# RMSNorm on one core: tiles two to four loaded whole, the first tile's store cut at row 1 and the second's at row 4

## The chip, the cores and the metric

The kernel runs on one core of a Trainium2 chip. The metric is the time of one execution on the device in microseconds (us). Three runs of the kernel before took 161.49, 161.64 and 162.53 us; the median, 161.64 us, is what the change is measured against.

The engines that matter here are ScalarE (ACT), VectorE (DVE), GpSimd (POOL), and SyncE (SP), which in this kernel does nothing but issue the transfers. All transfers go through SP's one queue to the core's 16 DMA engines. TensorE (PE) is used once, at the start.

## The reference

```python
def setup_inputs():
    batch, seq, dim = 16, 1024, 512
    return {
        "x": np.random.randn(batch, seq, dim).astype(np.float32),
        "gamma": np.ones(dim, dtype=np.float32),
    }

def reference(x: np.ndarray, gamma: np.ndarray) -> np.ndarray:
    eps = 1e-5
    rms = np.sqrt(np.mean(x ** 2, axis=-1, keepdims=True) + eps)
    return (x / rms * gamma).astype(np.float32)
```

Each of the 16,384 rows of 512 fp32 numbers is divided by its own root mean square and multiplied by gamma.

## The kernel before, in words

**Tiles, slots and rows.** The input is cut into four tiles of 128 partitions by 32 rows by 512 numbers, numbered 0 to 3 in the code ("the first tile" is tile 0). A partition holds 32 neighbouring rows of the input, so a tile is 64 KB in each partition. In what follows "a row" means one row in each of the 128 partitions: 256 KB. SBUF has room for three such tiles, `slot0` to `slot2`. The result is written over the input in place and stored from there. Tile 3 uses slot 0 again (`slot_of = [0, 1, 2, 0]`), so it can be loaded only when tile 0 has been stored. The profile does not tell slots or tiles apart: it writes `slot` for all three.

**Groups.** The list `groups` cuts the four tiles into nine groups of rows, (tile, first row, number of rows, pieces for the squares, rows given to POOL). A group's steps are these:

- `square_sums` (lines 96 and 97): ACT squares a piece of rows into scratch, DVE sums each row. Scratch is `sq_psum` (up to 7 rows) for even pieces, `sq_sbuf` (up to 5 rows) for odd ones. A piece of 9 rows goes to the last nine rows of slot 2 instead, which are free until tile 2 is loaded there.
- `inverse_rms` (lines 102 and 103): a square root on ACT, a reciprocal on DVE, for the whole group.
- `scale_by_pool` (lines 109 and 110): POOL multiplies the last rows of the group by the inverse and by gamma.
- `scale` (line 118): ACT multiplies the other rows by the inverse, one instruction a row, nine of a group of sixteen (thirteen in the last group).
- `times_gamma` (line 122): DVE multiplies these rows by gamma in one instruction.

**The order.** It is written out by hand; no scheduler changes it. The loop at the end works on group k and on the squares of group k+1 at once: on ACT the first two square pieces of the next group come first, then half of this group's scaling, then the third square piece if there is one, then the rest of the scaling. On DVE come the three sums of the next group, then `times_gamma` of this one, then the reciprocal of the next. Each engine runs its own list in order, so ACT, while it waits for data to square, does not scale the group before.

**Transfers.** `load` (line 45) and `store` (line 49) each issue one DMA on SP. SP runs its list in order too: a transfer whose wait is not over holds back all those behind it. Five loads are issued at the start (with gamma, in five small pieces, among them): tile 0 in rows 0:1, 1:8, 8:16 and 16:32, and the first half of tile 1. The others are issued by `transfers(t, g)`, called after `times_gamma` of group (t, g). A reader of loaded rows waits until the whole DMA that brings them has completed.

Of the kernel before, what the change touches and what calls it, by code (L numbers as in the profile page):

```python
# [9 lines left out]
def kernel(  # L10
# [33 lines left out]
    def load(t, slot, r0, r1):  # L44
        dma = nc.sync.dma_start(out=slots[slot][:, r0:r1], in_=xv[t][:, r0:r1])  # L45
        before_scale.append((slot, r0, r1, dma))

    def store(t, slot, r0, r1):
        dma = nc.sync.dma_start(out=ov[t][:, r0:r1], in_=slots[slot][:, r0:r1])
        before_scale.append((slot, r0, r1, dma))  # L50
# [6 lines left out]
    for c0, c1 in zip(pieces, pieces[1:]):  # L57
        nc.sync.dma_start(out=gamma_row[:, c0:c1], in_=gamma.unsqueeze(0)[:, c0:c1])
    load(0, 0, 8, 16)
    load(0, 0, 16, 32)  # L60
    load(1, 1, 0, 16)

    ones_col = const.tile([1, P], fp32)
    nc.gpsimd.memset(ones_col, 1.0)  # L64
# [11 lines left out]
    groups = [  # L76
        (0, 0, 7, (7,), 3),
        (0, 7, 9, (9,), 5),
        (0, 16, 16, (7, 9), 7),
        (1, 0, 16, (7, 9), 7),  # L80
        (1, 16, 16, (7, 5, 4), 7),
        (2, 0, 16, (7, 5, 4), 7),
        (2, 16, 16, (7, 5, 4), 7),
# [43 lines left out]
                tc.declare_no_dep(scaled.ins, earlier.ins, reason="ScalarE waited for it before it scaled these rows")  # L127

    def transfers(t, g):
        if (t, g) == (0, 0):  # L130
            store(0, 0, 0, 1)
            load(1, 1, 16, 32)
            store(0, 0, 1, 2)
            load(2, 2, 0, 23)
        elif (t, g) == (0, 16):
            store(0, 0, 2, 3)
            load(2, 2, 23, 32)
            store(0, 0, 3, 16)
            store(0, 0, 16, 32)
            load(3, 0, 0, 16)  # L140
            load(3, 0, 16, 32)
        elif (t, g) == (1, 16):
            store(1, 1, 0, 32)
        elif (t, g) == (2, 16):
            store(2, 2, 0, 32)
        elif (t, g) == (3, 0):
            store(3, 0, 0, 16)
        elif (t, g) == (3, 16):
            store(3, 0, 16, 32)
# [16 lines left out]
    for k, group in enumerate(groups):  # L166
        t, g, n, pieces, share = group
        mine = n - share
        half = (mine + 1) // 2
        ahead = groups[k + 1 :][:1]  # L170
        ss, todo = pieces_of(ahead[0]) if ahead else (None, [])
        scale_by_pool(rstd, t, g, n, share)
        for piece in todo[:2]:
            square_sums(*piece)
        scale(rstd, t, g, 0, half)
        for piece in todo[2:]:
            square_sums(*piece)
        scale(rstd, t, g, half, mine)
        times_gamma(t, g, 0, mine)
        transfers(t, g)  # L180
        for nxt in ahead:
            rstd = inverse_rms(ss, nxt[2])
# [30 lines left out]
```

## Time and profile before

| | |
|---|---|
| Median of three runs | 161.64 us |
| Span of the profiled execution | 160.2 us |
| DVE, ACT, POOL busy | 112.0, 107.8, 106.4 us |
| DMA queue of SP, packets and bytes | 2746, 67.11 MB |
| Its share of 16 DMA engines' span | 98.1% |
| Last DVE instruction ends | 139.1 us |
| Last store issued by SP, and its time to landing | 139.2 us, 20.1 us |

The span is the time from the first to the last instruction on the core in one profiled execution. The median of the runs is that of executions without a profile, and 1.4 us longer than the span. Only differences of the two kernels are compared, span with span, and the difference is laid on the median.

In the views that follow a line of the timeline has start, duration, engine, line of the code, operation, output <- input with shapes, and in brackets the idle time before it and what ended that. A line of several instructions (x4) has the time from the first one's start to the last one's end. A line of DMA issues has the number of transfers, KB of each, and microseconds from issue to landing where the profile could tell. For SP, the duration is that of issuing, not of the transfer.

### The profile page before, as it was taken

Reading aid. Unit: us, or ns where it says so; the run is one execution under the profiler, and the core shown is the slowest. Engines: PE = TensorE matmul, PEld = TensorE weight load, DVE = VectorE, ACT = ScalarE, POOL = GpSimd, SP = SyncE. Lnnn points to the kernel's source line nnn. Section 1 sums busy time; section 2 is a strip of 40 time slices with the busy share of each in tenths; the row PEclk is TensorE's granted clock in tenths of the full one; section 3 lists DMA queues with packets and bytes.
Section 4 is the critical chain, followed back from the end, with each engine's and each line's share of the span. In section 5 each row is a group of like instructions: output and inputs, shape, how many; then the busy total and the mean of one; then the engine's idle time right before and its main releaser. Section 6 shows DMA issues by size and latency. Waiting matters only on the chain.

```text
span 160.2 us, 276 instructions
## 1 busy us (share of the span) xinstructions
PE 2.0 (1%) x2; PEld 0.5 (0%) x2; DVE 112.0 (70%) x39; ACT 107.8 (67%) x108; POOL 106.4 (66%) x24
## 2 busy tenths in 40 slices
PE   0050000000000000000000000000000000000000
PEld 0010000000000000000000000000000000000000
DVE  0018098899798999999999999999999009700000
ACT  3071967976999998999899899989960990000000
POOL 1000951994999599999999999999999980000000
DMA  5999999899999899999999999996996996999994
GB/s 189 431 421 475 442 401 458 340 446 491 417 435 494 388 379 383 426 450 475 434 401 426 483 401 393 524 491 295 524 491 295 524 491 295 401 491 417 401 450 196
DMA packets 2747, 67.12 MB, mean 419 GB/s; under 512 B 313, under 2 KB 314, under 8 KB 826
## 3 DMA queue, kind: packets, MB, share of 16 engines
q1 hardware_dynamic: 2746, 67.11, 98.1%
q14 instruction: 1, 0.01, 0.0%
HBM read 33.56 MB, written 33.55 MB: 419 GB/s over the span
## 4 chain that ended last, share of the span: by engine, by line
DVE 59%; ACT 22%; DMA 4%; ACTq 0%; issue 0%; SPq 0%
DVE ss L97 36%; DVE slot L122 23%; ACT slot L118 8%; ACT slot L96 7%; ACT sq_psum L96 6%; DMA slot<-in_x_dram 4%; DVE ss L103 1%; ACT ss L102 1%; ACTq L208 0%; ACT gamma_b L165 0%; SPq L45 0%; ACTq L96 0%
## 5 line engine op out<-in xcount | busy, mean ns | idle before, releaser
L109 POOL TENSOR_TENSOR slot<-slot,ss 128x3584 f32<-128x3584 f32 (+2 forms) x9 | 47.0, 5218 | 24.1 <-DVE ss L103 24.1
L110 POOL TENSOR_TENSOR slot<-slot,gamma_b 128x3584 f32<-128x3584 f32 (+2 forms) x9 | 59.3, 6587 | 0.7
L97 DVE TENSOR_REDUCE ss<-sq_psum 128x7 f32<-128x3584 f32 (+1 forms) x13 | 42.2, 3247 | 13.7 <-ACT sq_psum L96 13.7
L118 ACT ACTIVATE slot<-slot,ss 128x512 f32<-128x512 f32 x75 | 47.3, 706 | 4.7 <-DVE ss L103 4.7
L122 DVE TENSOR_TENSOR slot<-slot,gamma_psum 128x4608 f32<-128x4608 f32 (+2 forms) x9 | 41.3, 4590 | 8.7 <-ACT slot L118 8.7
L96 ACT ACTIVATE sq_psum<-slot 128x3584 f32<-128x3584 f32 (+1 forms) x13 | 34.6, 2658 | 6.4 <-DMA slot<-in_x_dram 5.7
L97 DVE TENSOR_REDUCE ss<-slot 128x9 f32<-128x4608 f32 x3 | 14.9, 4954 | 4.4 <-ACT slot L96 4.2
L97 DVE TENSOR_REDUCE ss<-sq_sbuf 128x5 f32<-128x2560 f32 x5 | 14.0, 2803 | 0.0
L96 ACT ACTIVATE slot<-slot 128x4608 f32<-128x4608 f32 x3 | 12.1, 4033 | 0.0
L96 ACT ACTIVATE sq_sbuf<-slot 128x2560 f32<-128x2560 f32 x5 | 11.6, 2321 | 0.0
L102 ACT ACTIVATE ss<-ss,eps_t 128x16 f32<-128x16 f32 (+2 forms) x9 | 2.7, 305 | 11.9 <-DVE ss L97 11.9
L103 DVE RECIPROCAL ss<-ss 128x16 f32<-128x16 f32 (+2 forms) x9 | 2.1, 236 | 0.4 <-ACT ss L102 0.4
L66 PE MATMUL gamma_psum<-gamma_row,ones_col 1*128 1x512 f32 x2 | 2.0, 1122 | 8.6 <-DMA gamma_row<-in_gamma_dram 8.6
L72 ACT ACT_TABLE_LOAD x1 | 1.3, 1283 | 1.2 <-PEq L197 1.2
L165 ACT COPY gamma_b<-gamma_psum 128x512 f32<-128x512 f32 x1 | 0.6, 567 | 0.0
L66 PEld LDWEIGHTS gamma_psum<-gamma_row,ones_col 1*128 1x128 f32 x2 | 0.5, 308 | 8.6 <-issue 8.6
L64 POOL MEMSET ones_col<- 1x128 f32 x1 | 0.2, 195 | 0.3 <-POOLq L197 0.3
L197 POOL MEMSET const-float32-0.0<- 128x1 f32 x1 | 0.1, 99 | 0.2 <-issue 0.2
L72 ACT ACTIVATE table<-eps_t 128x1 f32<-128x1 f32 x1 | 0.2, 202 | 0.0
L197 POOL MEMSET const-bfloat16-1.0<- 128x1 bf16 x1 | 0.1, 102 | 0.0
L197 POOL MEMSET const-uint8-127<- 128x1 uint8 x1 | 0.1, 102 | 0.0
L197 POOL MEMSET const-float32-1.0<- 128x1 f32 x1 | 0.1, 99 | 0.0
(1 smaller groups left out, 0.1 us busy)
## 6 DMA issues: line engine op xcount, KB each, us to landing
slot<-in_x_dram SPq DMA_DIRECT2D x5, 4096.0 KB, 21.9
out_dram<-slot SPq DMA_DIRECT2D x3, 4096.0 KB, 23.4
slot<-in_x_dram SPq DMA_DIRECT2D x1, 5888.0 KB
out_dram<-slot SPq DMA_DIRECT2D x1, 3328.0 KB, 21.8
slot<-in_x_dram SPq DMA_DIRECT2D x1, 2304.0 KB, 14.3
slot<-in_x_dram SPq DMA_DIRECT2D x1, 2048.0 KB, 9.9
slot<-in_x_dram SPq DMA_DIRECT2D x1, 1792.0 KB, 7.0
out_dram<-slot SPq DMA_DIRECT2D x3, 256.0 KB
```

The costliest lines, as they stand in the source:

```text
L66: nc.tensor.matmul(gamma_psum[:, 0], ones_col, gamma_row, start=True, stop=True)
L72: nc.scalar.activation(out=table, in_=eps_t, func=AF.Sqrt)
L96: nc.scalar.activation(out=sq[:, :m], in_=rows, func=AF.Square)
L97: nc.vector.tensor_reduce(out=ss[:, r : r + m, 0], in_=sq[:, :m], axis=mybir.AxisListType.X, op=OP.add)
L102: nc.scalar.activation(out=ss[:, :n, 0], in_=ss[:, :n, 0], func=AF.Sqrt, bias=eps_t, scale=1.0 / D)
L103: nc.vector.reciprocal(out=ss[:, :n, 0], in_=ss[:, :n, 0])
L109: nc.gpsimd.tensor_tensor(out=part, in0=part, in1=by_row, op=OP.mult)
L110: last = nc.gpsimd.tensor_tensor(out=part, in0=part, in1=gamma_b.to_broadcast([P, share, D]), op=OP.mult)
L118: nc.scalar.activation(out=x[:, g + r, :], in_=x[:, g + r, :], func=AF.Copy, scale=rstd[:, r])
L122: scaled = nc.vector.tensor_tensor(out=part, in0=part, in1=gamma_psum.to_broadcast([P, r1 - r0, D]), op=OP.mult)
L165: nc.scalar.copy(out=gamma_b[:, 0], in_=gamma_psum[:, 0])
L197: nc = _bacc.Bacc("TRN2", target_bir_lowering=False, num_devices=1)
```

## The change

- The pair of half loads of tile 1, the two pieces of tile 2's load (rows 0:23 and 23:32) and the two half loads of tile 3 become one load of 32 rows each. Tile 1's load stays in the list at the start.
- Tile 0 was stored in rows 0:1, 1:2, 2:3, 3:16 and 16:32, with loads between them. It is now stored in row 0:1, issued after group (0, 7) and followed by tile 2's load, and in rows 1:32, issued after group (0, 16).
- After group (1, 0), rows 0:4 of tile 1 are stored, and behind that store stands the whole load of tile 3. The other 28 rows of tile 1 are stored after group (1, 16). Before, tile 1 was stored in one transfer of 32 rows.
- Groups (0, 16) and (1, 0) square their rows in pieces of 7, 5 and 4 instead of 7 and 9. Only group (0, 7) still uses the end of slot 2 as scratch.

The stores of tiles 2 and 3 are as before. There are 14 transfers of rows in place of 19.

```diff
     load(0, 0, 8, 16)
     load(0, 0, 16, 32)
-    load(1, 1, 0, 16)
+    load(1, 1, 0, 32)
...
         (0, 7, 9, (9,), 5),
-        (0, 16, 16, (7, 9), 7),
-        (1, 0, 16, (7, 9), 7),
+        (0, 16, 16, (7, 5, 4), 7),
+        (1, 0, 16, (7, 5, 4), 7),
         (1, 16, 16, (7, 5, 4), 7),
...
     def transfers(t, g):
-        if (t, g) == (0, 0):
+        if (t, g) == (0, 7):
             store(0, 0, 0, 1)
-            load(1, 1, 16, 32)
-            store(0, 0, 1, 2)
-            load(2, 2, 0, 23)
+            load(2, 2, 0, 32)
         elif (t, g) == (0, 16):
-            store(0, 0, 2, 3)
-            load(2, 2, 23, 32)
-            store(0, 0, 3, 16)
-            store(0, 0, 16, 32)
-            load(3, 0, 0, 16)
-            load(3, 0, 16, 32)
+            store(0, 0, 1, 32)
+        elif (t, g) == (1, 0):
+            store(1, 1, 0, 4)
+            load(3, 0, 0, 32)
         elif (t, g) == (1, 16):
-            store(1, 1, 0, 32)
+            store(1, 1, 4, 32)
         elif (t, g) == (2, 16):
             store(2, 2, 0, 32)
```

## The prediction

> **What bounds the kernel now.** I read the busy times first, then SP's list of issues, the transfers' times to landing, and last one steady stage of ACT and DVE.
>
> ```profile
> PE 2.0 (1%) x2; PEld 0.5 (0%) x2; DVE 112.0 (70%) x39; ACT 107.8 (67%) x108; POOL 106.4 (66%) x24
> DVE  0018098899798999999999999999999009700000
> ACT  3071967976999998999899899989960990000000
> DMA  5999999899999899999999999996996996999994
> q1 hardware_dynamic: 2746, 67.11, 98.1%
> ```
>
> No compute engine is busy for more than 70%, the transfers are for 98.1%, and they run on for 21 us after the last DVE instruction (139.14 us). The page's chain that ended last, which blames DVE for 59%, ends with that instruction; the span does not.
>
> ```profile
> 3.17 5.39 SPq L45 DMA_DIRECT2D slot<-in_x_dram  x3
> ...
> 49.83 0.33 SPq L45 DMA_DIRECT2D slot<-in_x_dram  x1
> 50.25 5.48 SPq L49 DMA_DIRECT2D out_dram<-slot  x2
> 72.09 10.27 SPq L45 DMA_DIRECT2D slot<-in_x_dram  x2
> 83.64 55.90 SPq L49 DMA_DIRECT2D out_dram<-slot  x4
> ```
> ```profile
> slot<-in_x_dram SPq DMA_DIRECT2D x1, 256.0 KB, 2.9
> slot<-in_x_dram SPq DMA_DIRECT2D x1, 4096.0 KB, 24.5
> slot<-in_x_dram SPq DMA_DIRECT2D x1, 2304.0 KB, 14.3
> out_dram<-slot SPq DMA_DIRECT2D x1, 4096.0 KB, 20.1
> ```
>
> The second block gives time to landing, in order: the first row (issued 0.74), tile 1's first half (issued 8.24), tile 2's last nine rows (49.83), the last store (139.20). Issue plus landing gives 32.7, 64.1 and 159.3 us for the last three. Between 64.1 and 159.3 the queue moved 157 rows in 8 transfers, between 32.7 and 64.1 it moved 51 rows in 6. With r us a row and c us a transfer, 157r + 8c = 95.2 and 51r + 6c = 31.4: **r = 0.599, c = 0.14**. A tile of 32 rows costs 19.3 us, a single row 0.74.
>
> An idle queue costs more: the first row landed 2.9 us after its issue, 2.3 more than 0.6 for its bytes. From the trace's packet and completion records I take the lower bound: first packets 1.0 us after the start of the issue, completion 0.36 us after the last packet, together 1.4. For issue plus completion in an idle queue I use 1.9, the middle.
>
> The last store, alone, would take 1.9 + 16 x 0.599 = 11.5 us. It took 20.1, so 8.6 us of it were queueing: **compute may be up to 8.6 us later than now for nothing**. That margin is what the change spends.
>
> ```profile
> 91.44 4.94 DVE L122 TENSOR_TENSOR slot<-slot,gamma_psum 128x4608 f32<-128x4608 f32 x1
> 91.77 3.14 ACT L96 ACTIVATE sq_psum<-slot 128x3584 f32<-128x3584 f32 x1
> 94.85 2.32 ACT L96 ACTIVATE sq_sbuf<-slot 128x2560 f32<-128x2560 f32 x1
> ...
> 97.08 3.16 ACT L118 ACTIVATE slot<-slot,ss 128x512 f32<-128x512 f32 x5
> ...
> 100.33 1.88 ACT L96 ACTIVATE sq_psum<-slot 128x2048 f32<-128x2048 f32 x1
> 102.14 2.54 ACT L118 ACTIVATE slot<-slot,ss 128x512 f32<-128x512 f32 x4
> ...
> 105.12 4.94 DVE L122 TENSOR_TENSOR slot<-slot,gamma_psum 128x4608 f32<-128x4608 f32 x1
> ```
>
> At 91.77 ACT squares the first rows of tile 3, whose first half was issued at 72.09 behind another store and, by the completion records, landed at 91.46: just in time. The line at 105.12 is `times_gamma` of (2, 16), behind the same ACT list.
>
> **The change part by part.**
>
> *Fewer transfers.* Nineteen become fourteen: 5 x 0.14 = 0.7 us less at most; none of the removed ones stood in an idle queue.
>
> *Pieces 7, 5, 4 for 7, 9 in two groups.* ACT 2.32 + 1.88 for 4.03, DVE 2.80 + 2.28 for 4.95: 0.3 us together per group, beside transfers, and absorbed by the wait for tile 1 that comes next. Cost nothing; without that cover 0.3 us a group.
>
> *Tile 1 whole.* Its first half landed at 32.7; all of it lands at 32.7 + 16 x 0.599 = 42.3. Group (1, 0) was first squared at 37.71, so ACT waits about 4.6 us, and scaling (0, 16) waits behind it. From the landing to the end of that group's `times_gamma` I take start-to-start times: 3.08 (squares of 7, 91.77 to 94.85), 2.23 (squares of 5, 53.52 to 55.75), 5 scalings at 0.613 (nine take 5.61, one 0.706), 1.81 (squares of 4, 100.33 to 102.14), 2.54, then DVE's 4.94: **17.7 us**. It ends at 60.0, when the 31-row store can be issued.
>
> The queue meanwhile holds the one-row store (0.74, SP free for it since 27.35) and tile 2 (19.3): 42.3 + 0.74 + 19.3 = 62.4. The store, issued at 60.0, needs 1.0 to 1.5 us to its first packet, so the queue does not run dry; 0.5 to 1 us is the margin. Tile 2 at 62.4 precedes its first use (64.40 plus the 4.6 just lost).
>
> *31 rows, four rows, tile 3.* The 31 rows land at 62.4 + 18.7 = 81.1. Tile 3's load waits for this landing, since it overwrites slot 0. The four rows of tile 1, issued after (1, 0) at about 74, fill 2.5 us meanwhile; the load needs 1.4 to 2.3. So it is covered, by 0.2 to 1.1 us, and uncovered it would cost the whole 1.9. Tile 3 lands at 81.1 + 2.5 + 19.3 = **102.9**.
>
> *What this late landing does.* ACT, ready for it at about 96.4 (91.77 + 4.6), waits until 102.9 with the scaling of (2, 16) behind the waiting squares. 17.7 us later, at 120.6, `times_gamma` of (2, 16) ends (before: 110.06). Only then can tile 2's store be issued. The queue has just tile 1's 28 rows left: 102.9 + 16.9 = 119.8. So **the queue runs dry**: issue at 120.7, plus 1.9, plus 19.2: landing at 141.8 instead of 139.1. Two half-tile stores of 9.7 follow: 161.2.
>
> The other bound: in the profile 29.08 us lie between the end of that `times_gamma` and the last one (110.06 to 139.14). All of it is ACT and DVE work that nothing shortens, so the last store is issued at 149.75 and lands at 149.75 + 1.9 + 9.6 = 161.3. Both meet. The same by the margin: 10.6 us later, 8.6 free, 2.0 paid. POOL stays behind its data: (3, 0)'s 14.0 us begin at about 120.8, and its part is done by 134.8, before its store's turn.
>
> *Sum.* Last landing 161.3 against 159.3: +2.0 us, and the span 162.2 against 160.2. On the median, which stands 1.4 us above the span: 161.64 + 2.0 = **163.6 us**, +1.2%.
>
> *Bounds.* The idle queue's 1.4 to 2.3: 0.5 either way. Tile 3's landing: with c at 0.07 (half the fit, were the earlier stretch slowed by something other than its transfers) 0.5 earlier; with 0.616 us a row, the earlier stretch's full mean (31.4/51), on all 116 rows after tile 1's first half, 32.7 + 71.4 = 104.1, 1.2 later.
>
> *Two rules weighed.* The row: a transfer in a full queue costs 0.14 us beyond its bytes. The Trainium skill's page "DMA: Bandwidth & Descriptors" (section "Anatomy of one DMA — SWDGE (gpsimd) path") gives each DMA a fixed cost of about 2.0 us for the other way of issuing, mostly completion. Charged to each of the five transfers, that would be an estimated gain of 10 us, and about 154 us for the kernel; the row says that back to back it is hidden.
>
> The row: ACT begins on tile 3 0.3 us after the landing of the half that it reads. Against the change speaks the same page's section "Why a DMA increments its semaphore by 16 and not by 1": only the full count means that all data landed, and a part of it doesn't tell which bytes have. By it a whole load has no usable first half; were the half usable, tile 3 would delay nothing after 93.3, and the time would be an estimated 161.
>
> **The rivals.**
>
> *Whole loads move faster, so the late landing shrinks (not slower).* Place: the three loads of 32 rows. No 32-row load stands in the trace; by the completion records tile 3's first half took 9.47 us after its forerunner, 0.592 a row, which would make a whole load 18.9 instead of 19.3. Three times 0.4 is 1.2 us by tile 3's landing: 101.7, and 162.4 us, +0.5%. Against it: the second half took 9.83. It decides from a gain of 0.4 us over the three, where the time falls below 163.26, 1% above the median; 1% is about what a measurement of this kernel tells from no change.
>
> *The hand-overs are not covered (slower still).* The four rows fill 2.5 us. If issue plus completion costs 3.0 with a store ending and a load starting, the queue is dry for 0.5 us ahead of tile 3, and 1.1 more than forecast ahead of tile 2's store: 165.2 us. For it: only one idle-queue start is in the trace. Against: that one cost 2.3 with everything cold.
>
> *ACT does not wait for the whole tile (the change then isn't what it says).* Only the fewer transfers count: 161.64 - 0.7 = 160.9 us. For it: nothing; the squares of (3, 0) wait for the one completion that the whole load has.
>
> **How the numbers follow.** The forecast 68%, faster loads 19%, uncovered hand-overs 11%, no wait 2%. Of the forecast's share about 6 points, with the idle queue near 1.4, lie below 163.26. Slower by over 1%: 0.62 + 0.11 = 0.73; within: 0.06 + 0.19 = 0.25; faster: 0.02, no case here reaching 160.02 but beyond its bounds. The range goes from 162.3 (the fast loads) to 165.2 (both upper bounds or the hand-overs).
>
> **What would show it.** Right: DVE's last instruction ends near 150; ACT sits idle some 4.6 us ahead of (1, 0) and some 6.5 ahead of (3, 0), both ended by `slot<-in_x_dram`; SP issues tile 3's load near 81 and tile 2's store near 121; the DMA row has a dip near 120 to 123 and none near 82; the last store lands about 11.5 us after its issue instead of 20.1. Wrong: a last store that still queues for several us, a DVE end before 148, or tile 3 landed by 101. A dip near 82 or near 62 would be the second rival.

## The result, and the profile after

The changed kernel took 165.51 us (median of four runs, 165.50 to 165.55), the kernel before in the same comparison 161.68: 3.8 us more, a ratio of 1.023 with a 95% interval of 1.021 to 1.026. The forecast was 163.6, with a range up to 165.2. The span of the profiled execution is 163.5 us against 160.2.

First the page of the changed kernel: busy times, the DMA row, SP's queue.

```profile
PE 2.0 (1%) x2; PEld 0.5 (0%) x2; DVE 112.4 (69%) x41; ACT 108.1 (66%) x110; POOL 106.4 (65%) x24
DMA  5999898997969959996998998999909959889885
q1 hardware_dynamic: 2026, 67.11, 96.4%
```

The engines do nearly the same work as before in a longer span, and the transfers' share falls from 98.1 to 96.4%. One slice of the DMA row, the thirtieth (118.5 to 122.6 us), is empty. A packet counts where it starts, so four windows show it more closely; their last two columns are the DMA share and GB/s, the third from last is TensorE's clock.

```profile
117.00:119.00 2.00, 0.00 (x0) 0.00 (x0) 1.81 (x2) 2.00 (x3) 0.00 (x0) 1.00 1.06 459
119.00:121.00 2.00, 0.00 (x0) 0.00 (x0) 2.00 (x1) 2.00 (x2) 0.00 (x0) 1.00 0.00 0
121.00:123.00 2.00, 0.00 (x0) 0.00 (x0) 2.00 (x3) 2.00 (x2) 0.58 (x1) 1.00 0.00 0
123.00:125.00 2.00, 0.00 (x0) 0.00 (x0) 2.00 (x1) 2.00 (x4) 2.00 (x1) 1.00 1.23 524
```

The packets that started just before 119 last 2.1 us, and the last of them ends at 120.99; none starts again before 123.07. For 2.1 us the queue moves nothing at all. Who let it run dry stands in the chain of waits in order of time (start, duration, what):

```profile
8.17 34.18 DMA slot<-in_x_dram
...
60.15 20.91 DMA out_dram<-slot
...
81.11 23.27 DMA slot<-in_x_dram
...
117.22 4.95 DVE slot L122
```

The chain runs through tile 1's load (landed at 42.35), the 31-row store (60.15 to 81.06), tile 3's load (81.11 to 104.38) and the `times_gamma` of (2, 16) that waits for ACT. The timeline shows the link between the last two:

```profile
96.32 0.31 ACT L102 ACTIVATE ss<-ss,eps_t 128x16 f32<-128x16 f32 x1 [0.56 <-DVE ss L97]
...
104.46 3.16 ACT L96 ACTIVATE sq_psum<-slot 128x3584 f32<-128x3584 f32 x1 [7.83 <-DMA slot<-in_x_dram]
...
117.22 4.95 DVE L122 TENSOR_TENSOR slot<-slot,gamma_psum 128x4608 f32<-128x4608 f32 x1 [0.19 <-ACT slot L118]
...
144.16 7.09 DVE L122 TENSOR_TENSOR slot<-slot,gamma_psum 128x6656 f32<-128x6656 f32 x1 [8.13 <-ACT slot L118]
```

ACT is through with the group before at 96.6 and sits idle for 7.83 us until the whole of tile 3 is there. Before, the line at 91.77 had no wait at all. DVE ends at 151.25 instead of 139.14.

SP's list and one of its landings (the store issued at 122.24; the number is microseconds to landing):

```profile
60.15 13.99 SPq L49 DMA_DIRECT2D out_dram<-slot  x2
81.11 0.34 SPq L45 DMA_DIRECT2D slot<-in_x_dram  x1
88.39 63.26 SPq L49 DMA_DIRECT2D out_dram<-slot  x4
```
```profile
out_dram<-slot SPq DMA_DIRECT2D x1, 20.8
```

Tile 2's store goes out at 122.24 and lands at 143.0, where it landed at 140.0 before. The last store, issued at 151.32, lands at 162.43 by the completion records, 3.1 us later than before.

### The profile page after: what moved, and what is told of

Same layout as the page of the kernel before. It is cut to its first block, busy times and chain, and to the rows that moved or that the text cites. A ratio compares the mean times of both kernels' runs of the same rounds, so it can differ in the third digit from the quotient of the medians.

```text
span 163.5 us, 267 instructions
## 1 busy us (share of the span) xinstructions
PE 2.0 (1%) x2; PEld 0.5 (0%) x2; DVE 112.4 (69%) x41; ACT 108.1 (66%) x110; POOL 106.4 (65%) x24
## 3 DMA queue, kind: packets, MB, share of 16 engines
q1 hardware_dynamic: 2026, 67.11, 96.4%
## 4 chain that ended last, share of the span: by engine, by line
DMA 52%; DVE 19%; ACT 18%; issue 2%; ACTq 0%; SPq 0%
DMA slot<-in_x_dram 39%; DVE slot L122 13%; DMA out_dram<-slot 13%; ACT slot L118 11%; DVE ss L97 5%; ACT sq_psum L96 4%; ACT sq_sbuf L96 3%; ACTq L204 0%; SPq L45 0%; DVE ss L103 0%; SPq L49 0%; ACTq L96 0%
## 5 line engine op out<-in xcount | busy, mean ns | idle before, releaser
L97 DVE TENSOR_REDUCE ss<-sq_psum 128x7 f32<-128x3584 f32 (+1 forms) x15 | 46.9, 3124 | 25.7 <-ACT sq_psum L96 25.7
L96 ACT ACTIVATE sq_psum<-slot 128x3584 f32<-128x3584 f32 (+1 forms) x15 | 38.3, 2554 | 19.6 <-DMA slot<-in_x_dram 18.2
L97 DVE TENSOR_REDUCE ss<-sq_sbuf 128x5 f32<-128x2560 f32 x7 | 19.6, 2805 | 0.0
L96 ACT ACTIVATE sq_sbuf<-slot 128x2560 f32<-128x2560 f32 x7 | 16.2, 2319 | 0.0
L97 DVE TENSOR_REDUCE ss<-slot 128x9 f32<-128x4608 f32 x1 | 5.0, 4955 | 4.2 <-ACT slot L96 4.2
L96 ACT ACTIVATE slot<-slot 128x4608 f32<-128x4608 f32 x1 | 4.0, 4042 | 0.0
## 6 DMA issues: line engine op xcount, KB each, us to landing
slot<-in_x_dram SPq DMA_DIRECT2D x1, 4096.0 KB, 18.9
```

The lines of the kernel that those rows point to most:

```text
L96: nc.scalar.activation(out=sq[:, :m], in_=rows, func=AF.Square)
L97: nc.vector.tensor_reduce(out=ss[:, r : r + m, 0], in_=sq[:, :m], axis=mybir.AxisListType.X, op=OP.add)
```

## The experiments

A load or store of rows is 128 packets, one for each partition, spread over the 16 DMA engines. Landings and packet times below come from the trace's completion and packet records. "Slow packets" means: recorded time above that of the other packets of the same size (2.42 us for 64 KB, 1.21 for 32 KB), summed and divided by the 16 DMA engines, so that it reads as delay of the whole queue. Every such figure is from one profiled execution. "Turn" has two senses: a transfer has its turn when the one ahead of it has landed, and the queue turns where it goes over from loading to storing or back. In the changed kernel tile 3's load had 0.48 us of slow packets at its first ones and 0.85 at its last, and took 20.84 us behind the four-row store instead of 19.3. The first theory, A, was: the time goes because ACT waits for the whole of tile 3, and part of that wait is slow packets where the queue turns between stores and loads.

**1. Tile 3 in halves again.**

```diff
-            load(3, 0, 0, 32)
+            load(3, 0, 0, 16)
+            load(3, 0, 16, 32)
```

> The changed kernel with tile 3 loaded in two halves again; all else as changed. Theory A (the time goes because ACT waits for the whole of tile 3, and 1.5 us of that wait come from slow packets where the queue turns between stores and loads): the first half lands near 93.5, before ACT is ready for it (96.4), so ACT waits only for tile 1 (4.7 us), the queue never runs dry after the start, the last store lands at 159.0 to 159.5 and the span is 160.0 to 160.5, time 161.4 to 162.2. Rival B (the cost sits in the whole loads of tiles 1 and 2 or in the merged stores of tile 0): the span stays above 162.

Measured: 163.06 us, ratio 1.007 (1.004 to 1.011), span 161.0. ACT's waits for loads, in the waits (total, times, longest):

```profile
ACT sq_psum L96 <- DMA slot<-in_x_dram: 10.3, 2, 5.5
```

Only the start (5.5) and tile 1 (4.8) are left of three waits with 18.2 us. The first half landed at 93.67, and the last store at 159.93 instead of 162.43. So **2.5 of the 3.1 us by which the last landing had moved come from loading tile 3 whole**, by way of ACT's wait; the time falls by 2.45 us, and 1.4 above the kernel before are left. It didn't come down to the expected 161.4 to 162.2: the two halves still took 20.8 us together, with 0.58 of slow packets early and 0.80 late. The slow packets are not a matter of the one long load.

**2. The kernel before, with tile 3 whole.**

```diff
-            load(3, 0, 0, 16)
-            load(3, 0, 16, 32)
+            load(3, 0, 0, 32)
```

> The kernel before with one part of the change alone: tile 3 loaded whole. Theory A: the load is issued when tile 0's second store has landed (82.0), the queue is dry for about 1.5 us, the last packets are slowed by the store queued behind it, and it lands near 103.7; ACT, ready at 91.8, sits idle for 12 us; the store of tile 1 (32 rows, 19.4 us) then covers nearly all of the 17.7 us to the next store, so the last landing is 161.7 to 162.2 and the time 164.0 to 164.6. Rival B: less than 162.4.

Measured: 165.58 us, ratio 1.022 (1.016 to 1.029), more than expected, and as much as the whole change. The chain of waits has the load:

```profile
81.46 23.02 DMA slot<-in_x_dram
```

It landed at 104.47, with slow packets of 0.76 us at the start (the queue was dry) and 1.05 at the end. This one edit alone is enough for the loss. The parts don't add up, though: without this edit the others still cost 1.4 us in the first experiment, and here the load is issued into a dry queue, which the changed kernel avoids.

**3. The 28-row store placed one group later.**

```diff
-        elif (t, g) == (1, 16):
+        elif (t, g) == (2, 0):
             store(1, 1, 4, 32)
```

> The changed kernel with the 28-row store of tile 1 issued one group later, after group (2, 0), at about 101.2 instead of 88.4, so that it is not queued while tile 3's load starts its last packets (99.9 to 100.6). Theory T (the load's last packets, 3.27 us instead of 2.42, are slowed by a store that already stands behind them): they take 2.42, tile 3 lands at 103.5 instead of 104.4, the queue does not run dry before the 28 rows, and the time falls by 0.8 us to about 164.7. Rival M (packets at that place are slow for another reason, of the memory or of the load's own length): the load still lands at 104.4 and the time is 165.5 or, if the later issue leaves a gap, more.

Measured: 165.50 us, ratio 1.022 (1.016 to 1.029), tile 3 landed at 104.36. This tells nothing of the theory: SP issued the store at 88.5 as before. SP waits for the data that a transfer needs, not for the place in the program where it stands; with nothing else in between, the edit moved nothing. It is a repeat of the changed kernel.

**4. No store ahead of tile 3's load.**

```diff
         elif (t, g) == (1, 0):
-            store(1, 1, 0, 4)
             load(3, 0, 0, 32)
         elif (t, g) == (1, 16):
-            store(1, 1, 4, 32)
+            store(1, 1, 0, 32)
```

> The changed kernel without the four-row store ahead of tile 3's load; tile 1 is stored in 32 rows after group (1, 16). Theory A: the queue is dry for about 1.6 us ahead of tile 3, the load lands near 102.8 (81.1 + 1.6 + 19.2 + 0.9 for the slowed last packets), 1.6 us earlier than in the changed kernel, and the 32 rows behind it (19.4 us) cover the way to tile 2's store, so the last landing is 160.9 to 161.4 and the time 164.0 to 164.5, faster than the changed kernel. Rival (the step as predicted: an uncovered hand-over costs its whole 1.9 us): 165.5 or more.

Measured: 165.41 us, ratio 1.022 (1.014 to 1.030): level with the changed kernel. That is 0.9 above theory A's range and 0.1 below the rival's least number, and the four runs (165.16 to 165.85) do not rule the rival out. The chain:

```profile
80.91 23.00 DMA slot<-in_x_dram
```

The load landed at 103.92, 0.46 earlier, not 1.6: theory A had allowed 0.9 us for slow packets, and they came to 0.74 and 1.05. With 32 rows behind it the queue did not run dry ahead of tile 2's store (tile 1's store landed at 123.24, tile 2's was issued at 121.78). The four rows move the dry time from one place to the other; they win nothing.

**5. The store behind tile 3 held back.**

```diff
-        elif (t, g) == (1, 16):
+        elif (t, g) == (2, 0):
+            store(2, 2, 0, 4)
             store(1, 1, 4, 32)
         elif (t, g) == (2, 16):
-            store(2, 2, 0, 32)
+            store(2, 2, 4, 32)
```

> The changed kernel with the first four rows of tile 2 stored after group (2, 0), ahead of the 28 rows of tile 1, and 28 rows of tile 2 after group (2, 16). SP waits for group (2, 0), so no store stands behind tile 3's load until about 101.2, when its last packets (from 99.9 on) are under way; and 32 rows instead of 28 then bridge the way to tile 2's store. Theory T (a store queued behind the load slows its last packets from 2.42 to 3.3 us): they take 2.42, tile 3 lands at 103.4 to 103.6, the queue does not run dry after it, the last landing is 161.5 to 162.0 and the time 164.4 to 164.9. Rival M (slow there for another reason): tile 3 lands at 104.3 to 104.5 again, and since the last store's issue then comes at 151.3, the time is 165.3 to 165.6.

Measured: 164.68 us, ratio 1.018 (1.011 to 1.025). Now SP really held the stores until 101.22. The chain:

```profile
81.16 21.93 DMA slot<-in_x_dram
```

Not one of the last packets was slow, and tile 3 landed at 103.09, 1.3 us earlier than in the changed kernel; the first packets were (0.38). The last landing moved from 162.43 to 161.14. In this execution it went as theory T has it (the load's last packets are slow when a store already waits behind them). But the four runs lie apart, 164.19, 164.24, 165.11 and 165.66 us, and the profiled one is the 164.24; the two others are nearer to rival M's 165.3 to 165.6. So the median gain of 0.8 us over the changed kernel is not firm, and theory T is supported here, not shown.

**6. Tile 3's hand-over as before, tiles 1 and 2 whole.**

```diff
         elif (t, g) == (0, 16):
-            store(0, 0, 1, 32)
-        elif (t, g) == (1, 0):
-            store(1, 1, 0, 4)
-            load(3, 0, 0, 32)
+            store(0, 0, 1, 16)
+            store(0, 0, 16, 32)
+            load(3, 0, 0, 16)
+            load(3, 0, 16, 32)
         elif (t, g) == (1, 16):
-            store(1, 1, 4, 32)
+            store(1, 1, 0, 32)
```

> The changed kernel with tile 3's hand-over as in the kernel before: tile 0 stored in rows 0:1, 1:16 and 16:32, tile 3 loaded in two halves behind them, tile 1 stored in one transfer; tiles 1 and 2 are still loaded whole. Theory J (a load that is issued only about 1 us before its turn pays 0.5 us at its first packets, and tile 3's load pays again at its end; one that is queued 10 us ahead pays neither): the first half lands near 91 and the second at 100.5 to 100.9, no slow packets over 0.3 us a DMA engine at either, the last store lands at 158.8 to 159.3 and the time is 161.5 to 162.0, level with the kernel before. Rival B (the whole loads of tiles 1 and 2 or the merged stores cost something by themselves): 162.5 or more.

Measured: 162.08 us, ratio 1.004 (1.000 to 1.007), the last landing at 159.01. The halves landed at 91.17 and 100.96, with less than 0.1 us of slow packets. The second half's issue (81.78) to landing:

```profile
slot<-in_x_dram SPq DMA_DIRECT2D x1, 4096.0 KB, 19.2
```

So the whole loads of tiles 1 and 2, tile 0's stores and the square pieces together cost 0.4%, and 0.7% at most. Theory J's landings held within 0.2 us, its time within 0.1. But 0.47 us of slow packets stand at the end of tile 2's load, where the changed kernel has none: the store behind it was issued at 39.4 here and at 60.15 there.

**7. Halves, behind eight rows.**

```diff
-            store(1, 1, 0, 4)
-            load(3, 0, 0, 32)
+            store(1, 1, 0, 8)
+            load(3, 0, 0, 16)
+            load(3, 0, 16, 32)
         elif (t, g) == (1, 16):
-            store(1, 1, 4, 32)
+            store(1, 1, 8, 32)
```

> The kernel of the first experiment (tile 3 in two halves) with eight rows of tile 1 stored ahead of them instead of four, so that the loads are issued at 81.1 but have their turn at 86, some 4.8 us later instead of 2.4. Theory J: the 0.5 us of slow first packets go, the two halves take 19.4 to 19.6 us plus what the last packets pay, and the time is 162.4 to 162.7, against 163.06 with four rows; if the slow last packets are a consequence of the slow start, they go too and the time is 161.7 to 162.0. Rival M (slow for a reason of that place): 163.0 again, with the halves taking 20.8 us together.

Measured: 163.02 us, ratio 1.009 (1.006 to 1.013): no gain, and rival M's time. The halves took 20.55 us; 0.48 us of slow packets stood at the end of the eight-row store and the beginning of the load, 1.1 at the load's end. Being issued about 5 us ahead of its turn instead of 2.4 did not help, against theory J.

**8. Two turns less.** Starting from the sixth:

```diff
         if (t, g) == (0, 7):
-            store(0, 0, 0, 1)
             load(2, 2, 0, 32)
         elif (t, g) == (0, 16):
-            store(0, 0, 1, 16)
-            store(0, 0, 16, 32)
-            load(3, 0, 0, 16)
-            load(3, 0, 16, 32)
+            store(0, 0, 0, 17)
+            store(0, 0, 17, 32)
+            load(3, 0, 0, 17)
+            load(3, 0, 17, 32)
```

> The kernel of the sixth experiment (tiles 1 and 2 whole, tile 3's hand-over as before) without the one-row store, and with tile 0 stored, and tile 3 loaded, in rows 0:17 and 17:32. So no store stands behind tile 1's load, and since row 16 is ready only at 60.1, none stands behind tile 2's load until its last packets are under way. Theory T (a store queued behind a load slows its last packets): the 0.3 us at the end of tile 1's load and the 0.5 us at the end of tile 2's go, the last landing is 158.0 to 158.5 and the time 161.0 to 161.5, against 162.08 for the sixth experiment: at or just below the kernel before (161.5). Rival M: the slow packets come back elsewhere and the time stays at 161.9 to 162.2.

Measured: 162.85 us, ratio 1.005 (1.002 to 1.009). Tiles 1 and 2 ended without slow packets, as theory T has it. But they came back around tile 3: 0.9 us on the way in, 0.8 on the way out, although its first half was issued at 71.85, 10 us ahead of its turn. Rival M's words, "come back elsewhere", fit better than mine, though the time lies above its range too.

**9. Four rows, but everything issued early.** Starting from the sixth:

```diff
             store(0, 0, 16, 32)
+        elif (t, g) == (1, 0):
+            store(1, 1, 0, 4)
             load(3, 0, 0, 16)
             load(3, 0, 16, 32)
         elif (t, g) == (1, 16):
-            store(1, 1, 0, 32)
+            store(1, 1, 4, 32)
```

> The kernel of the sixth experiment with four rows of tile 1 stored ahead of tile 3's two half loads, and 28 rows behind them, as in the changed kernel. The first half load is now issued at about 73.9 and has its turn at 84.2; in the first and seventh experiments it was issued 1 to 4 us ahead of its turn. Theory J (short notice is what makes tile 3's load slow, at its start and its end): the two halves take 19.4 to 19.8 us together, they land near 93.9 and 103.8, and the time is 161.9 to 162.4. Rival C (cutting tile 1's store around the load makes it slow): the halves take 20.5 us or more and the time is 162.9 or more.

Measured: 161.97 us, ratio 1.001 (0.998 to 1.004), level with the kernel before; the last landing at 158.89. SP's list and the two halves' times to landing (issued at 74.33 and 81.50):

```profile
39.60 34.62 SPq L49 DMA_DIRECT2D out_dram<-slot  x3
74.33 7.50 SPq L45 DMA_DIRECT2D slot<-in_x_dram  x2
88.50 55.90 SPq L49 DMA_DIRECT2D out_dram<-slot  x4
```
```profile
slot<-in_x_dram SPq DMA_DIRECT2D x1, 4096.0 KB, 19.3
```
```profile
slot<-in_x_dram SPq DMA_DIRECT2D x1, 4096.0 KB, 21.8
```

The halves took 18.95 us behind the four rows and had no slow packets, with tile 1's store cut in 4 and 28 rows as in the first experiment, which had 1.4 us of them. So neither that cut nor the place is the reason. What is left is when the transfers are issued, and that tile 0's store is in two pieces, which makes the early issue possible; the next experiment has these two pieces without it.

**10. A store kept waiting at tile 2's end.**

```diff
-            store(0, 0, 1, 32)
+            store(0, 0, 1, 16)
+            store(0, 0, 16, 32)
```

> The changed kernel with tile 0's 31 rows stored in two transfers, rows 1:16 and 16:32. The first can be issued at about 39.5, so a store stands in the queue when tile 2's load ends at 62, where the changed kernel has nothing waiting until 60.2. Tile 3 is still loaded whole, behind the same four rows, and issued about 3 us ahead of its turn. Theory N (what makes the later turns slow is that the queue had nothing waiting near 60 us; where a transfer always waits, as in the ninth experiment, the turn at tile 2's end costs 0.3 to 0.5 us and the later ones nothing): tile 3's load takes 19.2 to 19.6 us after the four rows, lands at 103.3 to 103.9, and the time is 164.3 to 164.8. Theory J (short notice of tile 3's own load): 20.5 us or more, landing at 104.6 or later, time 165.5 or more.

Measured: 166.09 us, ratio 1.029 (1.025 to 1.033), the slowest of all. Theory J was right on tile 3 here. The chain:

```profile
81.49 23.26 DMA slot<-in_x_dram
```

0.3 us of slow packets stand at tile 2's end, 0.3 at tile 3's start and 1.0 at its end; it landed at 104.76. The 31 rows in two pieces kept the queue filled at 60, and tile 3's own load, issued at 81.49 with its turn near 84.0, was slow all the same.

**11. No one-row store.** Starting from the sixth:

```diff
         if (t, g) == (0, 7):
-            store(0, 0, 0, 1)
             load(2, 2, 0, 32)
         elif (t, g) == (0, 16):
-            store(0, 0, 1, 16)
+            store(0, 0, 0, 16)
```

> The kernel of the sixth experiment without the one-row store: tile 0 stored in rows 0:16 and 16:32, tile 2's load directly behind tile 1's. A transfer always waits in the queue. Theory N: the 0.3 us at the end of tile 1's load go, the turn at tile 2's end costs 0.3 to 0.5, tile 3's turns nothing; last landing 158.3 to 158.8, time 161.2 to 161.7, level with the kernel before or just below it. Theory J, with tile 3's first half issued 10 us ahead of its turn, expects the same here. Rival M (a turn costs its half to one microsecond somewhere, whatever the order): 162.0 or more.

Measured: 162.15 us, ratio 1.003 (1.002 to 1.005). Tile 3's turns cost 0.1 us, but the end of tile 2's load 1.1, more than both turns there together in the sixth (0.3 and 0.5). That is rival M's time; theories N and J, which both expected 161.7 at most, are missed. With one turn less, the slow packets add up to more (1.2 us against 0.8 in the sixth).

**12. The eighth, with halves of 16 rows.**

```diff
-            store(0, 0, 0, 17)
-            store(0, 0, 17, 32)
-            load(3, 0, 0, 17)
-            load(3, 0, 17, 32)
+            store(0, 0, 16, 20)
+            store(0, 0, 0, 16)
+            store(0, 0, 20, 32)
+            load(3, 0, 0, 16)
+            load(3, 0, 16, 32)
```

> The kernel of the eighth experiment with tile 3 in halves of 16 rows again: tile 0 is stored in rows 16:20, 0:16 and 20:32, tile 3 loaded in rows 0:16 and 16:32 behind them. Rows 16:20 are ready at 60.1, so as in the eighth experiment nothing waits in the queue while tile 2's last packets begin; tile 3's first half is issued at about 74, 7 us ahead of its turn. Theory S (the eighth was slow at tile 3 because of its pieces of 17 and 15 rows): no slow packets over 0.3 us at tile 3's turns, last landing 158.0 to 158.6, time 161.0 to 161.6, level with the kernel before or just below. Theory N' (a queue with nothing waiting near 60 makes the later turns slow, whatever the pieces): 1.2 to 1.7 us of slow packets around tile 3's load, time 162.4 to 163.0.

Measured: 163.34 us, ratio 1.011 (1.009 to 1.012). 0.7 us of slow packets on the way into tile 3, 1.1 on the way out, though the first half was issued at 73.57 and had its turn near 81.8. SP's list, and the second half (issued 81.82), to be laid beside the 19.2 of the sixth:

```profile
59.82 1.77 SPq L49 DMA_DIRECT2D out_dram<-slot  x3
73.57 8.60 SPq L45 DMA_DIRECT2D slot<-in_x_dram  x2
88.11 55.89 SPq L49 DMA_DIRECT2D out_dram<-slot  x4
```
```profile
slot<-in_x_dram SPq DMA_DIRECT2D x1, 4096.0 KB, 20.4
```

Theory S falls; N' has the right sign and somewhat too small a number.

**All of them side by side.** The slow packets in us, at the end of tile 2's load, on the way into tile 3's load (with the end of the store ahead of it, and the first packets of a dry queue) and at its end. The second column is when, between 50 us and the end of tile 3's load, a transfer was issued less than 2.5 us ahead of its turn, or after it; all the others there were issued 3 us ahead or more, most of them 7 to 20.

| kernel | short notice at | end of tile 2 | into tile 3 | end of tile 3 |
|---|---|---|---|---|
| before | never | 0.4 | 0 | 0.2 |
| 6 | never | 0.5 | 0 | 0.1 |
| 9 | never | 0.3 | 0 | 0 |
| 11 | never | 1.1 | 0 | 0.1 |
| 10 | 81 | 0.3 | 0.3 | 1.0 |
| 2 | 81 (dry) | 0 | 0.8 | 1.0 |
| 7, 8, 12 | 60 | 0 | 0.5, 0.9, 0.7 | 1.1, 0.8, 1.1 |
| 1, after, 4 | 60 and 81 | 0 | 0.6, 0.5, 0.7 | 0.8, 0.9, 1.0 |
| 5 | 60, 81 and 101 | 0 | 0.4 | 0 |

Where every transfer was issued well ahead, tile 3's load lost 0.2 us or less; where one was issued on short notice, be it the load itself at 81 or tile 0's store at 60, it lost 1.3 to 1.8. The one exception, the fifth, held the next store back until the load's last packets had begun. This is read off these fourteen kernels (the third is the changed kernel again), and the rule as a whole was tried on no further one: the ninth and tenth were forecast from short notice of tile 3's load alone, the twelfth from nothing waiting near 60. Nor does the order of issue fix the cost. Up to tile 3's load the kernel before and the second experiment issue the same transfers, within 0.2 us of the same times, and the end of tile 2's load cost 0.4 us in the one and nothing in the other; the third, the repeat, paid 0.4 and 1.1 us at tile 3 where the changed kernel paid 0.5 and 0.9. The contrast between 0.2 and 1.3 us at tile 3 is larger than that. What the DMA engines do there is not shown: neither why a store issued late at 60 is paid for at 80 and 100, nor why the end of tile 2's load, with the store behind it issued early, cost between nothing (the second experiment) and 1.1 us (the eleventh).

None of the twelve beats the kernel before; the ninth is level with it.

## Why the prediction went wrong, by its own steps

- *Direction and mechanism held.* DVE's last instruction ended at 151.25 ("near 150"), ACT waited 4.7 us ahead of (1, 0) (4.6 forecast) and 7.8 ahead of (3, 0) (6.5), the DMA row has its dip near 120 and none near 82, and the last store landed 11.1 us after its issue (11.5). The half-tile experiment shows the mechanism from the other side: halves give 2.5 us back.
- *The steps up to tile 3 held within 0.15 us.* Tile 1 landed at 42.35 (42.3), the 31-row store was issued at 60.15 (60.0) and landed at 81.06 (81.1), the four rows at 83.54 (83.6).
- *The step that failed: "Tile 3 lands at 81.1 + 2.5 + 19.3 = 102.9".* It landed at 104.38, and ACT, DVE and the issue of the last store came later by as much. The term of 19.3 us for the whole load was 20.84. It was fitted on stretches of the kernel before, in which every transfer was issued 5 us or more ahead of its turn. I asked only whether the queue would run dry behind the four rows. It didn't, but the 31-row store and tile 3's load were issued about 2 us ahead of their turns, and in every kernel of the study with such a hand-over the load paid 1.3 us or more, the fifth excepted, which paid 0.4. In the changed kernel 1.35 of the 1.5 us are slow packets. Why short notice should cost this stays open.
- *The upper bound did not hold it.* With 0.616 us a row it put tile 3's landing at 104.1 at most; the records say 104.38.
- *The steps after it held.* From the landing to the end of `times_gamma` of (2, 16) 17.8 us passed (17.7), and 29.08 us lie between that end and the last one, as before. Issue plus completion in a drained queue was 1.6 us (20.8 less 19.2), within 1.4 to 2.3 and 0.3 below the value I took; that gave some of the error back. With 1.5 more and 0.4 less, 161.3 becomes the measured 162.4.
- *The median's base was 0.3 off.* I put the median 1.4 us above the span. Where both are listed, the runs of the kernel before show 1.73 to 1.83, so the profiled execution had probably taken about 161.9, slower than the median. The changed kernel's runs are 1.9 to 2.0 above their spans, and its span ends 1.06 us after the last landing instead of 0.83. These two differences, 0.4 us together, belong to no step, and their cause is open. So of the 1.9 us between the forecast 163.6 and the measured 165.5, 1.1 come from the late landing and some 0.7 from the base and the time outside the landings.
- *Rivals.* Faster whole loads: tiles 1 and 2 took 19.6 and 19.3 us, not 18.9, so no. Uncovered hand-overs: 165.2 lies closest to the measured time, but the place was wrong; the queue was never dry ahead of tile 3, and taking the four rows away altogether left the time level. That ACT would not wait for the whole tile is refuted by its 7.83 us.
- *The two rules of the Trainium skill, from the page "DMA: Bandwidth & Descriptors".* With the whole load ACT started 0.1 us after all of it had landed; with halves it never waited for tile 3. This agrees with the section "Why a DMA increments its semaphore by 16 and not by 1", by which only the full count means that all data landed. The sixth experiment, with four transfers fewer and tile 3 in halves, is 0.4% slower than before. Charging each of the five removed transfers the fixed 2.0 us that the section "Anatomy of one DMA — SWDGE (gpsimd) path" gives for the other way of issuing would have been an estimated gain of 10 us.

## What to carry to other kernels

A load is usable when all of it has landed, so the first piece that a reader waits for sets the size: before merging loads, lay the landing of the merged one beside the time at which its reader is ready, and compare the delay with the time that later stores spend queueing, which is the margin. A step that a busy queue hides is priced by the queue's state, not by its bytes alone: here a rate fitted on transfers that were all issued 5 us or more ahead did not hold where one was issued about 2 us before its turn, nor for those that followed it. And moving an issue in the program moved nothing where SP waited only for data (the third experiment).

## What the runs showed of the hardware

- The cost of turning from loading to storing and back was not a constant: from nothing to 1.1 us a turn, on packets that took up to 3.9 us instead of 2.42 (64 KB) or up to 2.2 instead of 1.21 (32 KB). It also differed by 0.4 us between two executions that had issued the same transfers up to there (the kernel before and the second experiment).
- Transfers of 64 KB in each partition ran at 2.42 us a packet on each of the 16 engines, 434 GB/s together, loads and stores alike.
- A store issued while the last packets of a load were already running left them at full speed (tile 2's end in the changed kernel, where the store was issued at 60.15; tile 3's in the profiled execution of the fifth experiment, where it was issued at 101.22).
